# Two head groups of a gated delta rule: one joint triangular solve, two recurrences advanced in turn, and the output projection dealt between the backward steps

## The chip, the cores and the metric

The kernel runs on one core of a Trainium2 chip. The metric is the device time of one execution in microseconds (us). Three timed runs of the kernel before gave 1509.27, 1511.0 and 1515.41 us, so the median is 1511.0 us. The engines are TensorE (PE, with its weight loads shown apart as PEld), VectorE (DVE), ScalarE (ACT), GpSimd (POOL) and SyncE (SP), which issues nearly all DMA transfers.

## The reference, cut to what matters

Two layers, each for 128 context tokens and 1024 latent tokens of width 1024. One input projection feeds three branches: A, windowed attention with 8 query heads over 2 key heads; B, a gated MLP over 128-token chunks; C, a gated delta rule in both directions, with 4 heads of width 64. The three are concatenated, projected by `w_out`, normalised, gated and added to the residual. All tokens of layer 1 depend on layer 0. Branch C is what the change is about:

```python
a_mat = where(strict, einsum('bnihd,bnjhd->bnhij', kb, k) * decay, 0)   # one 64x64 block per chunk and head
t_mat = triangular_solve(a_mat + eye, eye, lower=True, unit_diagonal=True)
u, w  = t_mat @ (v * beta), t_mat @ (kb * exp(gc))
def step(state, xs):                       # one chunk of 64 tokens after the other
    v_new = uc - wc @ state
    o     = qd @ state + aqk @ v_new
    state = state * exp(gl) + kd.T @ v_new
    return state, o
# forward over chunks 0..15, backward over chunks 15..0; the context has 2 chunks and its own states
o = o_forward + flip(o_backward);  o = rmsnorm(o) * silu(gate)
mix = concat(o_a, o_b, o_c) @ w_out;  y = x + gate * rmsnorm(mix)
```

## The kernel before, in words

One large function, `hybrid_trunk`, writes all instructions out. Tile tracks the dependencies and orders each engine's instructions when it builds the program; priority follows the order in which the code emits them, so emission order is the kernel's main means of scheduling. On the chip each engine executes its list in order.

**Chain and fill.** For each layer, `merge` (L1107) interleaves two Python generators. `chain()` is branch C: features and gates (`c_features`, `c_gates`), then `scan`. `fill()` is everything else: `b_branch`, `c_gate` (the projection that gates branch C), and `attention`; `both()` adds `b_gate` for two column halves. Each `yield` carries a number, about the TensorE time in us of what was just emitted; a chain yield is scaled by a factor from `SHARE` and by `FILL` = 0.9, and that much fill is emitted after it. For instance a query tile of attention yields 5.2, one head's scores 0.95, a key/value tile 2.9, a `b_branch` tile 3.2, a `b_gate` tile 2.75, a block of `c_gate` 5.2. Layer 0's fill also holds the modulation of layer 1 (`mod`).

**`scan` (L419).** The four heads go in two head groups `hg` of two. A block position `p` is a pair of chunks, 8 latent positions and one context position (`CTX`); `r` is 0 for the first half of a recurrence and 1 for the second. `prep` (L429) makes the decay-weighted products of one position in both directions. `diagonals` (L469), `solve` (L493) and `inverses` (L506) invert the 64x64 blocks: VectorE solves 32x32 triangles by 31 rank-one steps of two instructions (L500 multiplies, L502 subtracts), TensorE joins them. Order in a layer: context preps of both groups; 8 preps of group 0, with the context solve between them; the solve of group 0; the 18 steps of group 0, with the 8 preps of group 1 between them; the solve of group 1; the 18 steps of group 1. `b_gate` 0 is released inside the first latent solve and `b_gate` 1 inside the second (the list `light`).

**A step** (`pre` L552, `post` L565). `pre` scales and transposes the queries and keys (PSUM bank `psw`, one buffer). `post` holds the one buffer of bank `psv` from its first matmul (L572) to the last read of it: matmuls L572 and L573, the copy `vn` by VectorE (L575), matmuls L577, L580 and L581, the state update L585 by VectorE, and the output to `oacc` (L588 by ScalarE or L590 by VectorE). `prep` uses both banks too. In the second half (r = 1), group 1's steps end with `c_final_norm` and, a step later, `c_final_out`, which write their rows of the concatenated branches to `mix_d` in HBM.

**`out_layer` (L1027)** comes after `merge`. It loads the last two of the four column blocks of `w_out` (the first two are loaded at steps 6 and 8 of group 1), then for each of nine token tiles reads `OTm` from `mix_d` and does 96 matmuls of 256 columns (L1055), the norm, the residual and, in layer 0, the normalised input of layer 1 (`make_h`). Its tiles are emitted in the order 3, 4, 2, 5, 1, 6, 0, 7, 8: the middle tiles' positions are the first that the second half of the recurrences finishes.

PSUM has 8 banks: three of `psp`, and one each of a, b, c (`psw`), v (`psv`) and o.

Of the kernel before, what the change touches and what calls it, by code (L numbers as in the profile page):

```python
# [26 lines left out]
CTX = 8  # L27
# [4 lines left out]
SHARE = ((1.08, 5.56, 1.88, 2.27, 5.93, 1.0, 2.13), (1.39, 4.8, 2.03, 2.16, 2.49, 1.87, 1.7))  # L32
BOOST = 0

WO_AT = 6
# [5 lines left out]
LT = 9  # L41
AHEAD = 4
FILL = 0.9
# [3 lines left out]
def hybrid_trunk(  # L47
# [227 lines left out]
    def make_h(hp, xn, t, AB, first=False):  # L275
        cond = 1 if t == CTX else 0
        hf = hp.tile([128, 8, 128], F32, tag="hf", name=nm("hf"))
        for hh in range(2):
            ps = psb() if hh else psa()
# [139 lines left out]
    def scan(l, cqk, cv_, gates, oacc, ng, NAc, keep, wo, light):  # L419
# [9 lines left out]
        def prep(ep, hg, NA, p):  # L429
# [12 lines left out]
            V.tensor_copy(hl[:, 0, :, 0], hl[:, 1, :, 0])  # L442
            V.tensor_copy(hl[:, 0, :, 1], hl[:, 2, :, 0])
# [25 lines left out]
        def diagonals(ep, W, L):  # L469
            D = ep[:, 0:64 * L].rearrange("p (n c) -> p n c", c=32)  # L470
# [10 lines left out]
            M = ep[:, 1024:2048]  # L481
            Dt = D.transpose([0, 2, 1])
            Mt = M.rearrange("p (r c) -> p c r", c=32)
            if L < 16:
                Dt = bc(Dt, 2, 16 // L)
                Mt = Mt.rearrange("p c (x y) -> p c x y", y=2 * L)
            V.transpose(Mt, Dt)
            Y = ep[:, 2048:3072]
            V.memset(Y, 0.0)
            V.memset(Y[:, 0:1024:33], 1.0)  # L490
            return M, Y

        def solve(ep, M, Y):  # L493
            m3 = M.rearrange("p (r c) -> p r c", c=32)
            y3 = Y.rearrange("p (r c) -> p r c", c=32)
            for m in range(31, 0, -1):
                tmp = ep[:, 3072:3328]
                w = 32 - m
                t3 = tmp[:, 0:m * w].rearrange("p (r c) -> p r c", c=w)
                V.tensor_tensor(t3, m3[:, 0:m, m:m + 1].to_broadcast([128, m, w]),  # L500
                                y3[:, m:m + 1, m:32].to_broadcast([128, m, w]), op=ALU.mult)
                V.tensor_tensor(y3[:, 0:m, m:32], y3[:, 0:m, m:32], t3, op=ALU.subtract)  # L502
                yield 1.0


        def inverses(ep, W, L, Y):  # L506
            PQ = []
            for f in range(2):
                P_ = ep[:, 1024 * f:1024 * f + 1024].rearrange("p (a b) -> p a b", b=32)
                V.transpose(P_.transpose([0, 2, 1]), Y.rearrange("p (r c) -> p c r" if f == 0 else "p (r c) -> p r c", c=32))  # L510
                PQ.append(P_)
# [7 lines left out]
            C_ = ep[:, 3328:3840]  # L519
            S_.activation(C_[:, 0:32 * L], ps[:, 0:32 * L], AF.Copy, scale=-1.0)  # L520
# [18 lines left out]
        def steps(hg, NA, sp, fp):  # L539
# [3 lines left out]
            def scaled(r, p):  # L543
                e2 = eg[:, 0, r, p, h0:h0 + 2]
                qk = sp.tile([128, 2, 2, 64], F32, tag="qk", name=nm("qk"), bufs=3)
                G.tensor_tensor(qk, Cqk[:, p].rearrange("p k (h d) -> p k h d", d=64), bc(bc(e2, 1, 2), 3, 64), op=ALU.mult)
                kd = sp.tile([128, 2, 64], F32, tag="kd", name=nm("kd"), bufs=4)
# [4 lines left out]
            def pre(r, p, qk, kd):  # L552
# [8 lines left out]
                qw = sp.tile([128, 2, 2, 64], F32, tag="qw", name=nm("qw"))  # L561
                S_.copy(qw.rearrange("p k h c -> p (k h c)"), ps[:, 0:256])
                return qw, kd

            def post(r, p, S, pr):  # L565
# [8 lines left out]
                vn = sp.tile([128, 2, 64], F32, tag="vn", name=nm("vn"))  # L574
# [7 lines left out]
                Sd = sp.tile([128, 2, 64], F32, tag="Sd", name=nm("Sd"))  # L582
                G.tensor_tensor(Sd, S, bc(eg[:, 2, r, p, h0:h0 + 2], 2, 64), op=ALU.mult)
                Sn = sp.tile([128, 2, 64], F32, tag="S", name=nm("S"), bufs=4)
# [8 lines left out]
            def swap(S):  # L593
                Sn = sp.tile([128, 2, 64], F32, tag="S", name=nm("Sx"), bufs=4)
                dma(Sn[0:64], S[64:128])
                dma(Sn[64:128], S[0:64])
                return Sn

            Sl = sp.tile([128, 2, 64], F32, tag="S", name=nm("S0"), bufs=4)
            for d in range(2):  # L600
                dma(Sl[64 * d:64 * d + 64], state_delta[0, l, d, h0:h0 + 2].rearrange("h d v -> d h v"))
            Sc = sp.tile([128, 2, 64], F32, tag="S", name=nm("Sc"), bufs=4)
# [655 lines left out]
```

## Time and profile before

| | before |
|---|---|
| median of three runs | 1511.0 us |
| the profiled execution, its own time | 1512.14 us |
| its span, first to last instruction | 1510.3 us |
| TensorE busy | 1324.8 us (88%) |
| VectorE busy | 971.8 us (64%) |
| ScalarE / GpSimd busy | 658.0 / 651.4 us |
| mean granted TensorE clock | 0.931 of full speed |

The profile is of one execution. Its page gives each engine's busy time, the wait before each group of instructions and what ended it, and the chain of work that ended last. A busy TensorE is not TensorE at its densest: the end of a matmul is modelled, and sparse small matmuls can count as busy. So the windows, which give the number of matmuls in a stretch beside the busy time, say more than the share on the page.

### The profile page before, as it was taken

The page shows a single profiled execution, that of the slowest core. Times are in us where ns is not written, and L with a number is a line of the kernel's source. Part 1 is how long each engine was busy: PE and PEld are TensorE (multiplying, and loading weights), DVE is VectorE, ACT ScalarE, POOL GpSimd, SP SyncE. Part 2 cuts the span into 40 slices and gives each one's busy share as a digit, 9 for nine tenths or more (in the row PEclk, how much of TensorE's full clock was granted, in tenths as well). Part 3 has the DMA queues.
Part 4 walks back from the last instruction along what each step waited for, and adds up shares of the span by engine and source line. Part 5 has one row for each costly group of instructions (what it writes and reads, how often), then busy time and mean ns, then how long its engine had stood idle before and what let it go on. Part 6 is the DMA issues. An engine that isn't in the chain of part 4 may idle for free.

```text
span 1510.3 us, 38004 instructions
## 1 busy us (share of the span) xinstructions
PE 1324.8 (88%) x15191; PEld 1014.2 (67%) x15191; DVE 971.8 (64%) x2446; ACT 658.0 (44%) x1483; POOL 651.4 (43%) x890
## 2 busy tenths in 40 slices
PE   6899978799988598888989998889987779977997
PEld 2764565566657487667877655778776668855887
DVE  2855789986556575764555766979765385756333
ACT  2733445624555315642443444443566314654211
POOL 0751156624565423662324335553566413656200
PEclk8999999999999889989998998999997789988999
DMA  9331044537864215666332112341556112756443
GB/s 357 104 93 37 23 105 121 125 116 189 170 163 88 42 50 122 114 174 171 128 114 60 58 36 83 83 102 40 96 113 95 34 52 64 143 94 164 128 156 110
DMA packets 301563, 162.91 MB, mean 108 GB/s; under 512 B 212622, under 2 KB 277938, under 8 KB 301386
## 3 DMA queue, kind: packets, MB, share of 16 engines
q1 hardware_dynamic: 301261, 160.45, 43.1%
q8 instruction: 119, 1.95, 0.5%
q14 instruction: 58, 0.48, 0.1%
q10 hardware_dynamic: 125, 0.04, 0.0%
HBM read 95.78 MB, written 24.28 MB: 79 GB/s over the span
## 4 chain that ended last, share of the span: by engine, by line
PE 48%; DVE 21%; DMA 12%; issue 7%; POOL 5%; ACT 5%; SPq 1%; DVEq 0%; POOLq 0%; ACTq 0%
PE ps L170 13%; PE ps L1055 11%; PE ps L312 7%; DMA PT<-P 4%; DMA st<-in_w_in_dram 3%; DVE sv L502 2%; DVE sv L500 2%; PE ps L249 2%; POOL P L934 2%; DVE sS L927 2%; PE ps L950 1%; DVE wg L161 1%; PE ps L533 1%; PE ps L517 1%; PE ps L698 1%
## 5 line engine op out<-in xcount | busy, mean ns | idle before, releaser
L170 PEld LDWEIGHTS <-X 128*128 128x128 f16 x3888 | 352.5, 101 | 108.4 <-issue 43.8
L170 PE MATMUL ps<-wg,X 128*128 128x256 f16 x2592 | 331.1, 281 | 14.8 <-DVE wg L161 4.4
L1055 PEld LDWEIGHTS <-OTm 128*128 128x128 f16 x1728 | 170.4, 100 | 38.1 <-DMA OTm<-mix_d 13.9
L934 POOL TENSOR_TENSOR P<-sS,P 128x512 f16<-128x512 f32 (+2 forms) x144 | 150.1, 1048 | 87.7 <-ACT sS L932 69.9
L1055 PE MATMUL ps<-wo,OTm 128*128 128x256 f16 x1296 | 155.1, 280 | 13.3 <-DMA OTm<-mix_d 12.7
L312 PE MATMUL ps<-X,wg 128*128 128x512 f16 (+1 forms) x864 | 145.7, 328 | 1.8 <-ACT wg L160 1.4
L931 ACT ACTIVATE P<-sS,nmx 128x512 f16<-128x512 f32 (+2 forms) x144 | 93.4, 659 | 89.6 <-DVE nmx L929 78.2
L312 PEld LDWEIGHTS <-wg 128*128 128x128 f16 x864 | 73.8, 99 | 68.5 <-ACT wg L160 1.8
L170 PE MATMUL ps<-wb,X 128*128 128x256 f16 x864 | 105.7, 284 | 12.2 <-DVE wb L161 6.2
L927 DVE CUSTOM_DVE_ANT_0 sS<-ps,am 128x512 f32<-128x512 f32 (+2 forms) x144 | 86.1, 609 | 35.2 <-PE ps L923 18.3
L950 PE MATMUL ps<-Vt,PT 128*128 128x128 f16 (+1 forms) x992 | 72.3, 215 | 34.5 <-DMA PT<-P 30.1
L932 ACT ACTIVATE sS<-sS,nmx 128x512 f32<-128x512 f32 (+2 forms) x144 | 94.7, 658 | 4.0
L145 POOL TENSOR_TENSOR rs<-ms,mhalf 128x1 f32<-128x1 f32 x36 | 19.8, 552 | 167.8 <-DVE ms L1064 89.7
L950 PEld LDWEIGHTS <-PT 128*128 128x128 f16 x992 | 51.9, 102 | 52.8 <-DMA PT<-P 43.7
L319 DVE SCALAR_TENSOR_TENSOR y<-zT,cw,y 128x1156 f32<-128x1156 f32 x48 | 68.9, 1438 | 28.3 <-ACT y L317 27.7
L502 DVE TENSOR_TENSOR sv<-sv 128x31 f32<-128x31 f32 (+15 forms) x186 | 77.3, 415 | 4.0
L500 DVE TENSOR_TENSOR sv<-sv 128x31 f32<-128x31 f32 (+15 forms) x186 | 74.0, 398 | 3.8
L923 PE MATMUL ps<-KT,qT 128*128 128x128 f16 (+2 forms) x272 | 71.2, 277 | 0.0
L922 PE MATMUL ps<-KT,qT 128*128 128x128 f16 (+2 forms) x272 | 62.3, 278 | 7.5 <-DMA qT<-ql 4.5
L161 DVE SCALAR_TENSOR_TENSOR wg<-st,wg 128x1024 f16<-128x1024 f32 x44 | 55.2, 1261 | 18.0 <-ACT wg L160 17.9
L160 ACT ACTIVATE wg<-st 128x1024 f16<-128x1024 f32 x44 | 45.2, 1054 | 46.3 <-DMA st<-in_w_in_dram 30.3
L1058 ACT ACTIVATE sq<-ps 128x512 f32<-128x512 f32 x36 | 21.3, 593 | 98.6 <-PE ps L1055 56.9
(272 smaller groups left out, 2861.9 us busy)
## 6 DMA issues: line engine op xcount, KB each, us to landing
st<-in_w_in_dram SPq DMA_DIRECT2D x40, 512.0 KB
st<-in_w_mod_dram SPq DMA_DIRECT2D x32, 512.0 KB
OTm<-mix_d SPq DMA_DIRECT2D x18, 512.0 KB
wm<-in_w_mod_dram SPq DMA_DIRECT2D x16, 512.0 KB
xt<-in_x_sample_dram SPq DMA_DIRECT2D x16, 512.0 KB
st<-in_w_out_dram SPq DMA_DIRECT2D x16, 512.0 KB
mix_d<-OTA SPq DMA_DIRECT2D x36, 128.0 KB
xs<-xt SPq DMA_DIRECT2D x9, 512.0 KB
```

What stands on the lines that cost most here:

```text
L161: V.scalar_tensor_tensor(dst[:, 4 * h:4 * h + 4, 1, :cols], s, WS, hi, op0=ALU.mult, op1=ALU.subtract)
L170: T.matmul(ps, X[:, t, k, a, :], wg[:, k, b, c0:c0 + n], start=(i == 0), stop=(i == 23))
L312: T.matmul(ps[:, 0:n], wg[:, k, b, 128 * hg:128 * hg + 128], X[:, t0:t1, k, a, :], start=(i == 0), stop=(i == 23))
L500: V.tensor_tensor(t3, m3[:, 0:m, m:m + 1].to_broadcast([128, m, w]), y3[:, m:m + 1, m:32].to_broadcast([128, m, w]), op=ALU.mult)
L502: V.tensor_tensor(y3[:, 0:m, m:32], y3[:, 0:m, m:32], t3, op=ALU.subtract)
L923: T.matmul(ps[:, cs], qT[:, h, :], Kl[:, kv, ks], start=False, stop=True)
L927: V.tensor_tensor_reduce(sS[:, 0:nk], ps[:, 0:nk], mk, 1.0, NEG, ALU.add, ALU.max, accum_out=mx[:, h:h + 1])
L931: S_.activation(P16[:, 0:nk], sS[:, 0:nk], AF.Exp, bias=nmx[:, h:h + 1], scale=0.125)
L932: S_.activation(sS[:, 0:nk], sS[:, 0:nk], AF.Exp, bias=nmx[:, h:h + 1], scale=0.125, accum_out=sm[:, h:h + 1])
L934: G.tensor_tensor(P16[:, nk:2 * nk], sS[:, 0:nk], P16[:, 0:nk], op=ALU.subtract)
L950: T.matmul(pops[:, 128 * h:128 * h + n], PT[:, a * nb + j, :], Vt[:, blist[j], kv].rearrange("p s d -> p (s d)")[:, 0:n], start=(i == 0), ...
L1055: T.matmul(ps[:, 256 * i:256 * i + 256], OTm[:, k, a, :], w[:, k, b, :], start=(n == 0), stop=(n == 23))
```

## The change

`scan` now does all 18 preps in a row (groups alternating), with the context solve between them. One `solve` runs both groups' latent blocks at once: its tiles have a further dimension of two, it has 30 rank-one steps instead of 31, and it works in place on the negated matrix (the sign moves into the copies at the head of `prep`), so that the separate result and its full memset are gone. `diagonals` and `inverses` still run once per group. Then the steps of both groups are emitted in turn, one of each per yield, 18 pairs. Each group has its own tags for its step tiles; banks c and v stay single. Context steps come first in each half.

`out_layer` becomes a generator at the end of the fill. A tile may be emitted once its positions are in the list `done`, which `c_final_out` fills; before that the generator yields `None`, and `merge` caps its credit at 6. The context tile goes first. All of `w_out` is loaded at its start. `c_gate` and both `b_gate` halves are the fill from the end of the preps on, and `merge` emits what is left of them before the steps begin. `SHARE` and `FILL` get new values, and the second buffer of `GG` goes.

```diff
-SHARE = ((1.08, 5.56, 1.88, 2.27, 5.93, 1.0, 2.13), (1.39, 4.8, 2.03, 2.16, 2.49, 1.87, 1.7))
+SHARE = ((1.08, 7.4, 2.1, 8.4), (1.39, 5.9, 2.1, 7.9))
-FILL = 0.9
+FILL = 1.0
...
-            V.tensor_copy(hl[:, 0, :, 0], hl[:, 1, :, 0])
+            V.tensor_scalar(hl[:, 0, :, 0], hl[:, 1, :, 0], -1.0, None, op0=ALU.mult)
...
+        def solve(Y, tmp, n):
+            y = Y.rearrange("p (s r c) -> p s r c", s=n, c=32)
+            for m in range(30, 0, -1):
+                w = 31 - m
+                t = tmp[:, 0:n * m * w].rearrange("p (s r c) -> p s r c", s=n, c=w)
+                V.tensor_tensor(t, y[:, :, 0:m, m:m + 1].to_broadcast([128, n, m, w]),
+                                y[:, :, m:m + 1, m + 1:32].to_broadcast([128, n, m, w]), op=ALU.mult)
+                V.tensor_tensor(y[:, :, 0:m, m + 1:32], y[:, :, 0:m, m + 1:32], t, op=ALU.add)
+                yield 1.0
...
+                    for i in range(16):
+                        prep(gp, i % 2, NAs[i % 2], i // 2)
+                        for _ in range(2):
+                            next(ctx_solve, None)
+                        yield share[1]
...
+                light.append(1)
+                for hg in range(2):
+                    diagonals(D[:, 1024 * hg:1024 * hg + 1024], Y[:, 1024 * hg:1024 * hg + 1024], Ws[hg], 16)
+                yield 4.0
+                for cost in solve(Y, D, 2):
+                    yield cost * share[2]
...
+                light.append(2)
+                yield 4.0
...
+                both = [steps(hg, NAs[hg], sp, fp, oacc) for hg in range(2)]
+                for _ in range(18):
+                    for s in both:
+                        next(s)
+                    yield share[3]
...
-            for ti, t in enumerate((3, 4, 2, 5, 1, 6, 0, 7, 8)):
+            for ti, t in enumerate((8, 3, 4, 2, 5, 1, 6, 0, 7)):
+                while not all(p in done for p in ((CTX,) if t == CTX else (min(2 * t, 15 - 2 * t), min(2 * t + 1, 14 - 2 * t)))):
+                    yield None
...
-                    g = p1.tile([128, DM], F32, tag="GG", name=nm("GG"), bufs=2)
+                    g = p1.tile([128, DM], F32, tag="GG", name=nm("GG"), bufs=1)
...
-                    ps = psp() if ti % 2 == 0 else (psw() if hh else psb())
+                    ps = psa() if ti % 2 and hh else psp()
...
-            while credit > 0:
-                c_ = next(fill, None)
+            while credit > 0 or len(light) == 2:
+                c_ = next(fill, -1)
                 if c_ is None:
-                    credit = -1e9
+                    credit = min(credit, 6.0)
+                    break
...
+            todo = [c_gate, lambda l, bp: b_gate(l, bp, 0), lambda l, bp: b_gate(l, bp, 1)]
```

## Rows read from the trace of the kernel before

**Rows 1.** The page's first part: busy us of each engine, share, instructions.

```profile
PE 1324.8 (88%) x15191; PEld 1014.2 (67%) x15191; DVE 971.8 (64%) x2446; ACT 658.0 (44%) x1483; POOL 651.4 (43%) x890
```

**Rows 2.** Windows of 20 us: busy (instructions) of five engines, clock, DMA.

```profile
1180.00:1200.00 20.00, 14.38 (x226) 12.56 (x224) 7.56 (x27) 4.91 (x13) 9.32 (x19) 0.57 0.18 34
1460.00:1480.00 20.00, 20.00 (x186) 17.93 (x184) 6.15 (x14) 2.75 (x8) 1.08 (x2) 1.00 0.54 172
...
400.00:420.00 20.00, 20.00 (x261) 13.78 (x259) 10.74 (x34) 10.07 (x28) 12.72 (x17) 1.00 0.76 165
```

**Rows 3.** Timeline of one step of layer 1: start us, us, engine, line.

```profile
1200.08 0.33 PE L580 MATMUL ps<-S,qw 64*64 64x64 f32 x4
...
1200.19 0.33 PE L581 MATMUL ps<-vn,NA 64*64 64x64 f32 x4
...
1206.09 0.34 PE L572 MATMUL ps<-cv,NA 64*64 64x64 f32 x4
...
1208.55 0.28 DVE L590 TENSOR_TENSOR oacc<-oacc,ps 128x128 f32<-128x128 f32 x1
```

**Rows 4.** The same windows, by stage of each layer.

```profile
75.00:205.00 130.00, 120.83 (x1048) 72.72 (x1046) 84.35 (x109) 53.13 (x90) 38.90 (x35) 0.99 0.21 57
205.00:306.00 101.00, 84.02 (x825) 61.54 (x824) 87.26 (x243) 53.52 (x142) 64.34 (x99) 0.92 0.52 123
306.00:377.00 71.00, 67.81 (x735) 47.53 (x737) 55.13 (x142) 27.02 (x60) 26.11 (x30) 0.95 0.58 149
377.00:521.00 144.00, 123.54 (x1830) 91.70 (x1822) 80.65 (x255) 75.12 (x186) 81.37 (x128) 0.97 0.55 119
521.00:577.00 56.00, 50.56 (x611) 43.66 (x612) 41.42 (x98) 12.24 (x23) 11.11 (x11) 0.86 0.19 54
577.00:663.00 86.00, 71.55 (x1188) 57.61 (x1187) 56.87 (x180) 52.73 (x132) 56.79 (x80) 0.94 0.65 122
663.00:795.00 132.00, 118.39 (x1195) 102.91 (x1193) 69.00 (x176) 49.20 (x93) 37.69 (x48) 0.95 0.50 152
795.00:926.00 131.00, 127.70 (x1107) 82.88 (x1105) 91.33 (x128) 54.97 (x88) 46.34 (x37) 0.95 0.21 59
926.00:1025.00 99.00, 87.92 (x868) 69.63 (x869) 77.34 (x199) 45.66 (x112) 54.45 (x89) 0.93 0.32 81
...
1092.00:1217.00 125.00, 98.23 (x1558) 79.37 (x1557) 65.73 (x206) 65.09 (x158) 73.44 (x119) 0.83 0.45 78
...
1281.00:1386.00 105.00, 88.99 (x1360) 71.56 (x1359) 69.94 (x221) 63.16 (x161) 68.59 (x93) 0.91 0.64 118
1386.00:1511.00 125.00, 109.25 (x1094) 94.45 (x1091) 44.48 (x104) 21.55 (x55) 15.55 (x24) 0.95 0.47 144
```

**Rows 5.** Groups of VectorE by line and shape: count, busy us, mean ns, idle before.

```profile
L465 DVE TENSOR_TENSOR NA<-ps,E 128x256 f32<-128x256 f32 x64 | 23.8, 412 | 13.4 <-POOL E L463 10.0 <-PE ps L454 3.3
L442 DVE COPY PK<-PK 128x128 f16<-128x128 f16 x36 | 10.2, 283 | 19.6 <-ACT PK L438 19.4
L500 DVE TENSOR_TENSOR sv<-sv 128x31 f32<-128x31 f32 x12 | 2.3, 194 | 0.2
L500 DVE TENSOR_TENSOR sv<-sv 128x256 f32<-128x256 f32 x6 | 3.2, 526 | 0.1
L510 DVE STREAM_TRANSPOSE sv<-sv 128x1024 f32<-128x1024 f32 x12 | 23.5, 2014 | 0.1
```

**Rows 6.** Windows of the state update L585 alone: one per step.

```profile
588.00:704.00 116.00, 5.08 (x18) 0.93 0.69 153
1296.00:1422.00 126.00, 5.05 (x18) 0.91 0.62 131
```

**Rows 7.** Timeline of the last step of layer 1 and the next output tile.

```profile
1421.06 0.28 DVE L590 TENSOR_TENSOR oacc<-oacc,ps 128x128 f32<-128x128 f32 x1
...
1437.68 1.15 PE L1055 MATMUL ps<-wo,OTm 128*128 128x256 f16 x7 [3.66 <-DMA OTm<-mix_d]
```

More of the change, by code (lines that the diff above doesn't have):

```diff
@@ L275, in make_h @@
     def make_h(hp, xn, t, AB, first=False):
+        hb = (lambda: psa()) if first else (lambda: bank("o", 1))
         cond = 1 if t == CTX else 0
@@ L416, in c_gates, with scan @@
         yield 6.0
-    def scan(l, cqk, cv_, gates, oacc, ng, NAc, keep, wo, light):
+    def scan(l, cqk, cv_, gates, ng, NAc, light, done):
         GB, eg, kdf, gh, gl = gates
@@ L617, in steps @@
                     if r == 0:
-                        Sc = swap(Sc)
+                        Sc = swap(Sc, p)
+                    else:
+                        for d in range(2):
+                            dma(new_s[0, l, 1 - d, h0:h0 + 2].rearrange("h d v -> d h v"), Sc[64 * d:64 * d + 64])
                 else:
@@ L640, in scratch @@
-        def scratch(p, tag=None):
-            return p.tile([128, 4096], F32, tag=tag, name=nm("sv")) if tag else p.tile([128, 3840], F32, name=nm("sv"))
-        def lat_solve(hg, sv):
-            M, Y = diagonals(sv, Ws[hg], 16)
-            yield 4.0
-            for i, cost in enumerate(solve(sv, M, Y)):
-                if i == (2 if hg else LT):
-                    light.append(hg)
-                yield cost * share[5 if hg else 2]
-            inverses(sv, Ws[hg], 16, Y)
-            yield 4.0
@@ L653, in scan @@
-        blocks(hp, "na")
-        with pool(f"gx{l}", 1) as cx, pool(f"gp{l}0", 2) as gp:
-            for i in range(2):
-                prep(gp, i, None, CTX)
-                yield share[1]
-            cx = scratch(cx)
-            M, Y = diagonals(cx, Wc, 4)
-            ctx_solve = solve(cx, M, Y)
-            for p in range(8):
-                prep(gp, 0, NAs[0], p)
-                for _ in range(4):
-                    next(ctx_solve, None)
-                yield share[1]
-            inverses(cx, Wc, 4, Y)
@@ L667, in scan @@
-        with pool(f"gv{l}", 1) as gv:
-            yield from lat_solve(0, scratch(gv))
-        hp1 = keep.enter_context(pool(f"ge{l}", 1))
-        blocks(hp1, "nb")
-        with pool(f"gp{l}1", 2) as gp, pool(f"gs{l}0", 2) as sp:
-            for i, cost in enumerate(steps(0, NAs[0], sp, None)):
-                cost *= share[3]
-                if i % 2 and i < 16:
-                    prep(gp, 1, NAs[1], i // 2)
-                    cost += share[4]
-                yield cost
-        yield from lat_solve(1, scratch(hp, "na"))
@@ L1105, in hybrid_trunk, with merge @@
             make_h(ph, xts[t], t, AB, True)
-    def merge(chain, fill):
+    def merge(chain, fill, light):
         credit = 0.0
@@ L1155, in chain @@
                     yield cost * SHARE[l][0]
-            yield from scan(l, cqk, cv_, gates, oacc, ng, NAc, keep, wo, light)
+            for cost in scan(l, cqk, cv_, gates, ng, NAc, light, done if OUTM else later):
+                yield cost
+            done.extend(later)
+        later = []
         def fill():
@@ L1160, in fill @@
                 yield from b_branch(l, vt, bp)
-            with pool(f"cg{l}", 1, "right") as cgp:
-                yield from c_gate(l, cgp)
             if l + 1 < NL:
@@ L1188, in hybrid_trunk @@
                 next(fl)
-        merge(chain(), fl)
+        merge(chain(), fl, light)
         rs.close()
-        out_layer(l, wo, nxt[1])
-        keep.close()
         ls.close()
```

168 lines of the change are left out of this document (82 added, 86 removed).

## The prediction, made before the changed kernel was run

> **What bounds the kernel now.** I read the page's first part, then windows cut at the stages of each layer, then the timeline of single steps. The page says TensorE is busy 88% of the span and VectorE 64% [rows 1], which looks like a kernel with 12% left to win. The windows say more. Where output tiles run alone, 186 matmuls of 256 columns fit in 20 us [rows 2]: 107.5 ns each, TensorE at its densest. The small fp32 matmuls of a step, issued closely, come four in 0.12 us, or 29 ns each [rows 3]. Giving every matmul of a stretch the dense time of its shape (107.5 ns per 256 columns and in proportion, 29 ns for the small ones) turns counts into "dense work": 1165 us for all 15,191, which is 77% of the span, against 88% busy. The rest, some 345 us, is room.
>
> By stage, dense work over length of the window [rows 4] is:
>
> - features: 119 of 130 us in layer 0, 123 of 131 in layer 1, so 0.92 and 0.94
> - first preps: 72 of 101 (0.71) and 79 of 99 (0.80). VectorE is busy 87 of the 101
> - latent solves, with `b_gate` beside them: 65 of 71 (0.91) and 45 of 56 in layer 0. Layer 1's stand between its rows' ends, 67 and 64 us long, at 0.84 and 0.81
> - steps of group 0 with the preps of group 1: 101 of 144 (0.70) and 66 of 125 (0.53)
> - steps of group 1: 56 of 86 and 67 of 105, both about 0.65
> - output, with the last steps still running: 110 of 132 (0.83) and 102 of 125 (0.82)
>
> The losses sit in the two stages of steps: 73 us in layer 0, 97 us in layer 1. Their worst form is a recurrence whose fill has run out. At 1180 to 1200 us TensorE is called busy for 14.4 us, holds 7 us of dense work, and has a granted clock of 0.57 of full speed, part of it at 1.2 GHz instead of 2.4 [rows 2]. The best form is attention rich in query tiles, 20 of 20 us busy at 400 to 420, 0.87 by dense work [rows 2]. No engine is full over the whole span; each stage loses to waits between small instructions, and what decides is whether the program has other matmuls to put there.
>
> On the 88%: the Trainium skill ("Perfetto Trace Analysis", Identifying the Most-Contended Engine) says that matmul busy is a poor measure of distance to the peak and that weight-load busy is a better one. Here weight loads are busy 67% [rows 1]. By the matmul share at most 185 us could be won, by the weight-load share 496; the 345 above lies between, and my sum goes by stages and needs neither.
>
> **The change part by part.** All matmuls stay, so I redistribute about 566 us of dense work per layer and give each new stage the density of the old stage most like it. Fill is counted in the yields' own us: 5.2 for a query tile is 48 matmuls x 107.5 ns.
>
> *Prologue*: unchanged, 75 us.
>
> *Features.* `c_gate` (23 us of dense work) leaves, key/value tiles and `b_branch` come in by credit: six features and 14 of gates at 1.08 give 22 of fill in layer 0, 28 at 1.39 in layer 1. The chain's own work is about 85. So 107 / 0.92 = 116 us and 113 / 0.93 = 121 us.
>
> *Preps.* 18 in a row, at 7.4 and 5.9: 133 and 106 of fill. A prep is about 1.0 us of TensorE (8 transposes and 14 products of 64 or 128 columns). Layer 0: 18 + 4 for the context inverses + 133 = 155 of dense work. VectorE: two copies of 0.3 and two L465 of 0.41 [rows 5] make 1.45 per prep, 26 us; the context solve 24 us (60 instructions of about 0.4, between the two rows of L500 [rows 5]); its transposes 8. The first preps before held ten preps, the context solve and 50 of fill in 87 us of VectorE [rows 4], which leaves 0.8 us per unit of fill, so 133 units need 106. Sum 164 us. VectorE is the tighter one here: at the 0.86 that it reached before, 190 us. Layer 1: 128 of dense work at 0.80 is 160 us, VectorE 134 / 0.86 = 156; I take 160. The negating copies replace plain copies of the same shape; a gain or loss of 0.1 us on 72 is 7 us either way and lies under the same 0.86.
>
> *Solve.* Instructions of 31 and 256 elements take 194 and 526 ns on average [rows 5]: 0.15 us and 1.48 ns per element. Two solves before: 124 instructions, 21,824 elements, 51 us. The joint one: 60 instructions, 19,840 elements, 38 us. With diagonals and inverses (three transposes of 2.0 us [rows 5] and some smaller copies per group) VectorE needs about 56 us. TensorE has 73 of fill (`c_gate` and both `b_gate` halves, all of which must be out before the steps) and 16 of joining matmuls: 89 / 0.90 = 99 us. So the solve, whatever it saves on VectorE, is hidden behind the gate projections; the two stages before took 127 and 131. Without that cover it would cost the 56.
>
> *Steps.* 36 turns per layer, 28 matmuls in two passes each: 56 x 29 ns = 1.6 us per turn. Bank v is still one buffer, so the groups take turns in it; a turn holds it from 1206.09 to 1208.83 [rows 3], about 3 us with little else on the engines. Under load, 18 steps took 116 and 126 us [rows 6], 6.4 and 7.0 us each. Side by side therefore buys no shorter chain by itself; what it buys is one place for all fill. Per pair 8.4 or 7.9 of fill go with 3.2 of steps, against 1.9 and 1.6 before in group 1's stage. First half: what is left of attention, 61 and 83, plus 28 of steps: 89 / 0.70 = 127 us and 111 / 0.70 = 159 us. That is 7.1 and 8.8 us per turn, at or above the rows.
>
> *Second half and output.* 94 of output tiles, 28 of steps, 4 of transposes: 126 / 0.83 = 152 us per layer, tail included. I keep the output stage's old density: tiles are dense and always ready, but after the last step norm, write and read of `mix_d` stay, 16.6 us from the last `oacc` to the next tile's first matmul [rows 7]. The loads of `w_out` are the same eight halves as before, now together after attention; the recurrences run beside them. Single-buffered `GG` delays one tile's epilogue, not its matmuls: nothing, as the next tile's 10 us cover it.
>
> *Sum.* Layer 0: 116 + 190 + 99 + 127 + 152 = 684 us (720 before, 75 to 795). Layer 1: 121 + 160 + 99 + 159 + 152 = 691 us (716 before). With 75 the span is 1450 us, 60 under 1510.3. The execution lay 1.8 us above its span and 1.1 us above the median, so against the median of 1511.0 I forecast **1450 us**, 4.0% less.
>
> **Bounds of the unknown.** No row shows attention beside two recurrences or output tiles beside backward turns from the start. First half: 0.53 to 0.87 gives 377 to 230 us for both layers against 286, so +91 to -56. Second half: 0.64 to 0.94 gives 394 to 268 against 304, so +90 to -36. Preps: 0.71 in both layers is +48; VectorE at 0.95 is -25. I take the middle densities because the fill per turn is four times that of the stages at 0.65, yet attention's own waits stay.
>
> **Rivals.**
>
> *Turns in one bank (slower).* If two recurrences and denser fill stretch a turn, the chain sets the steps' time. My sum allows 279 and 311 us for 36 turns, 7.8 and 8.6 us each. For it: 6.4 to 7.0 us per turn were reached with a quarter of the fill [rows 6]. Against it: a bare turn is 3 us. At 10 us per turn the steps take 720 us instead of 590, so 1580 us; slower than before from 9.1 us per turn on.
>
> *Tiles block the list (no gain).* A tile's matmuls stand in TensorE's list behind the step that frees them; if the read has not landed, both recurrences wait behind it. 16.6 us less a pair's 8.4 of fill is 8.2 us at four points in two layers: +66, 1516 us. For it: TensorE idled 3.66 us at such a point [rows 7]. Against it: the order is made from an estimate of readiness. The Trainium skill ("TensorE: Matmul & The Clock Gate", Step-by-step: what each phase is for) says that matmuls stay in program order while only weight loads are pulled ahead; by that rule nothing behind such a matmul could run. The row agrees as far as it goes: no other matmul ran in that gap.
>
> *Denser throughout (faster still).* First half 0.87, second 0.94: 1358 us. For it: the stretch at 400 [rows 2]. Against it: no long stretch with attention kept that.
>
> *It does not do what it says.* Tile may order the groups one after the other again, and the output last. Only the joint solve and the moved gates would stay, about 1505 us.
>
> **Chances.** Forecast, 1405 to 1495: 0.56. Denser, below 1405: 0.12. Blocked tiles, 1495 to 1519: 0.09, half of it under 1503. Not as said: 0.05. Turns, above 1519: 0.18. A difference under 0.5%, 7.5 us, can hardly be told from none. Faster 0.73, same 0.09, slower 0.18. The range is 1390 to 1525 us: it leaves about 0.05 below and 0.15 above.
>
> **What would show it.** Right: L585 in pairs, 13 to 17 us per pair; the joint L500 near 0.9 us at its widest; matmuls of the output tiles between L585 of the second half; TensorE at clock 1.0 through it; about 10 us of output matmuls alone per layer at the end. Wrong: gaps before L572 that bank v ends, or before L1055 that `OTm` ends, or VectorE full through the solve with TensorE waiting.

## The result and the profile after

The changed kernel takes 1581.98 us (median of four runs, 1579.81 to 1587.09) against 1510.43 us before on the same chip: a ratio of 1.0472, 95% interval 1.0437 to 1.0507. The forecast was 1450 us. The matmuls keep their form, but lines shift: the tile matmul L1055 is L1047 now, a step's L572, L577 and L585 are L569, L574 and L582, the solve's L500 is L495.

The page's first part answers [rows 1]: busy us of each engine, share of the span, instructions.

```profile
PE 1341.5 (85%) x15191; PEld 1026.5 (65%) x15191; DVE 955.8 (61%) x2308; ACT 657.2 (42%) x1483; POOL 663.8 (42%) x890
```

The same matmuls are called busy 17 us longer in a span 68 us longer. The windows of the changed kernel, one for each term of the sum (features, preps, solve, first half, second half with output, for layer 0 and then layer 1), answer [rows 4]; after the busy times of five engines stand clock, DMA share and GB/s.

```profile
75.00:232.00 157.00, 138.48 (x1217) 92.16 (x1216) 100.59 (x164) 63.64 (x129) 68.83 (x71) 0.92 0.26 67
232.00:385.00 153.00, 128.61 (x1264) 82.02 (x1262) 122.53 (x352) 96.86 (x230) 91.25 (x128) 0.94 0.73 167
385.00:525.00 140.00, 127.79 (x1381) 99.92 (x1381) 81.77 (x175) 40.65 (x91) 33.92 (x40) 0.90 0.32 84
525.00:649.00 124.00, 100.97 (x1692) 83.46 (x1690) 75.47 (x220) 69.96 (x174) 71.60 (x107) 0.93 0.65 128
649.00:855.00 206.00, 164.16 (x1918) 139.82 (x1919) 82.26 (x228) 54.31 (x109) 56.57 (x86) 0.86 0.29 87
855.00:1003.00 148.00, 133.35 (x1194) 91.97 (x1193) 102.89 (x151) 61.06 (x109) 68.32 (x65) 0.96 0.22 58
1003.00:1140.00 137.00, 111.47 (x1209) 87.95 (x1208) 118.19 (x340) 88.92 (x218) 88.43 (x130) 0.93 0.40 78
1140.00:1265.00 125.00, 111.23 (x1237) 87.26 (x1235) 84.13 (x163) 41.04 (x85) 33.09 (x30) 0.83 0.35 91
1265.00:1397.00 132.00, 118.49 (x1849) 100.08 (x1846) 71.16 (x227) 64.90 (x174) 74.92 (x118) 0.96 0.48 89
1397.00:1578.00 181.00, 152.46 (x1892) 127.71 (x1892) 72.10 (x193) 39.33 (x101) 47.24 (x74) 0.92 0.41 119
```

Set against the sum, both layers together: features and preps 595 us, forecast 587 (+8); solve 265, forecast 198 (+67); first half 256, forecast 286 (-30); second half and output 387, forecast 304 (+83). These make the 128 us between 1450 and 1578, the span. Dense work, counted as in the prediction, is 132 of 206 us (0.64) and 128 of 181 us (0.70) in the last stage, where 0.83 was assumed.

What such a stage looks like is in the timeline of TensorE in layer 0: start, duration, line; in brackets the idle time before and what ended it.

```profile
698.23 0.33 PE L578 MATMUL ps<-vn,NA 64*64 64x64 f32 x4
704.57 4.24 PE L1047 MATMUL ps<-wg,OTm 128*128 128x256 f16 x24 [6.01 <-DMA OTm<-mix_d]
708.65 2.78 PE L1047 MATMUL ps<-wo,OTm 128*128 128x256 f16 x24
...
719.13 2.78 PE L1047 MATMUL ps<-wo,OTm 128*128 128x256 f16 x24
721.84 0.34 PE L569 MATMUL ps<-cv,NA 64*64 64x64 f32 x4
```

A step ends at 698.6. Next in TensorE's order stand six blocks of 24 tile matmuls, and the first waits 6 us for its read of `mix_d`, whose rows of branch C an earlier step had to finish. The next step starts at 721.84. In between, neither recurrence moves, and so no new position is finished: tile and step take turns instead of overlapping. The first block after the gap takes 4.24 us, the others 2.78. At the end the last tile waits for the last step. The tail of layer 0 answers [rows 7]. TensorE idles 8.4 us before L281, the transposes with which `make_h` turns a finished tile into layer 1's input: with no other tile free they stand next in its order, and wait for that tile's norm.

```profile
814.95 0.44 PE L716 MATMUL ps<-ident,on 128*128 128x128 f32 x2 [0.23 <-DVE hf L288]
823.79 1.97 PE L281 MATMUL ps<-ident,xn 128*128 128x128 f32 x8 [8.41 <-ACT xn L272]
826.17 4.87 PE L1047 MATMUL ps<-wg,OTm 128*128 128x256 f16 x24 [0.41 <-DMA OTm<-mix_d]
```

The chain that ended last shows that this idle time lies inside a longer wait: the read of the last tile, issued behind the write of its rows, lands just before that tile's first matmul (start, length, step of the chain).

```profile
820.00 1.82 DMA mix_d<-oc
821.84 4.28 DMA OTm<-mix_d
```

Before that, once attention had run out (its last matmul ran at 624) and until the first tile was free (670), both recurrences ran bare; this window, with the first tile in it, answers the first of [rows 2]:

```profile
613.00:700.00 87.00, 57.58 (x970) 48.73 (x969) 33.76 (x90) 25.21 (x57) 31.31 (x59) 0.80 0.41 109
```

It holds 37 us of dense work in 87, 10 of them the first tile, at a granted clock of 0.80: part of it at 1.2 GHz.

### The profile page after: what moved, and what is told of

It reads as the page before. It is cut to its first block, busy times and chain, and to the rows that moved or that the text cites. A ratio compares the mean times of both kernels' runs of the same rounds, so it can differ in the third digit from the quotient of the medians.

```text
span 1578.0 us, 37851 instructions
## 1 busy us (share of the span) xinstructions
PE 1341.5 (85%) x15191; PEld 1026.5 (65%) x15191; DVE 955.8 (61%) x2308; ACT 657.2 (42%) x1483; POOL 663.8 (42%) x890
## 5 line engine op out<-in xcount | busy, mean ns | idle before, releaser
L169 PE MATMUL ps<-wg,X 128*128 128x256 f16 x2592 | 324.8, 278 | 12.6 <-DVE wg L160 5.8
L921 POOL TENSOR_TENSOR P<-sS,P 128x512 f16<-128x512 f32 (+2 forms) x144 | 154.3, 1078 | 133.1 <-ACT sS L919 89.8
L1047 PEld LDWEIGHTS <-OTm 128*128 128x128 f16 x1728 | 172.3, 101 | 51.4 <-DMA OTm<-mix_d 24.6
L312 PE MATMUL ps<-X,wg 128*128 128x512 f16 (+1 forms) x864 | 151.6, 335 | 17.4 <-ACT vf L991 9.5
L1047 PE MATMUL ps<-wg,OTm 128*128 128x256 f16 x864 | 114.8, 292 | 22.6 <-DMA OTm<-mix_d 22.6
L1047 PE MATMUL ps<-wo,OTm 128*128 128x256 f16 x864 | 103.1, 274 | 0.0
L160 DVE SCALAR_TENSOR_TENSOR wg<-st,wg 128x1024 f16<-128x1024 f32 x44 | 58.5, 1343 | 35.5 <-ACT wg L159 35.4
L540 POOL TENSOR_TENSOR qk<-cqk,eg 128x256 f32<-128x256 f32 x72 | 46.0, 639 | 48.4 <-PE ps L553 48.3
L495 DVE TENSOR_TENSOR sv<-sv 128x168 f32<-128x168 f32 (+28 forms) x120 | 64.8, 540 | 1.6
```

Of the source, the lines that this page charges most:

```text
L169: T.matmul(ps, X[:, t, k, a, :], wg[:, k, b, c0:c0 + n], start=(i == 0), stop=(i == 23))
L312: T.matmul(ps[:, 0:n], wg[:, k, b, 128 * hg:128 * hg + 128], X[:, t0:t1, k, a, :], start=(i == 0), stop=(i == 23))
L495: V.tensor_tensor(t, y[:, :, 0:m, m:m + 1].to_broadcast([128, n, m, w]), y[:, :, m:m + 1, m + 1:32].to_broadcast([128, n, m, w]), op=ALU.mult)
L921: G.tensor_tensor(P16[:, nk:2 * nk], sS[:, 0:nk], P16[:, 0:nk], op=ALU.subtract)
L1047: T.matmul(ps[:, 256 * i:256 * i + 256], OTm[:, k, a, :], w[:, k, b, :], start=(n == 0), stop=(n == 23))
```

## Experiments

Each kernel was timed beside the kernel before on the same chip; the number in parentheses is its ratio to before with the 95% interval. Unless said otherwise the edit is made on the changed kernel (1582 us).

**Is it the dealing?** Three edits: tiles after all steps, steps ahead of the tiles in the list, and tiles that wait for nothing.

```diff
-OUTM = 1
+OUTM = 0        # `done` is filled only after all 36 steps are emitted
```

> Changed: the dealing alone is undone. An output tile is released only when all 36 steps have been emitted, so in the lists every step comes before every tile unless the scheduler finds a gap for the tile. Theory A (list order): dealt tiles stand in TensorE's list as whole blocks of 96 matmuls ahead of the next steps, so tiles and steps take turns instead of overlapping; the second half with the output took 215 and 190 us after against 154 and 153 before, and this should win back 60 to 100 us of these 98: 1480 to 1520 us. Theory B (late tiles): the tiles come late because a tile now needs the second half of both groups, and the recurrences run bare before that; no order of the list helps: 1570 to 1600 us.

Measured: 1539.72 us (1.0191, 1.0159 to 1.0222). 42 us come back, less than expected of theory A and more than of B. Dealing is one loss among others.

```diff
-BOOST = 0
+BOOST = 400
...
-            tc.cur_priority = at - BOOST
+            ahead = BOOST if len(light) == 3 else 0
+            tc.cur_priority = at - ahead
...
-            tc.cur_priority += BOOST
+            tc.cur_priority += ahead
```

> Changed: the instructions of the steps get a priority 400 places ahead of the fill that was emitted before them; the dealing stays. In TensorE's list steps then stand inside the blocks of tile matmuls, mostly one step to 40 or 50 matmuls. Theory A (list order): 60 to 100 us less, 1480 to 1520 us, like the kernel without dealing. Theory B (late tiles): 1570 to 1600 us.

Measured: 1567.5 us (1.0379, 1.034 to 1.0418), 15 us less. Steps now stand inside the blocks, and the idle time before tiles is still 14.9 us (22.6 in the changed kernel, 12.7 before). Order of the list alone is not enough.

```diff
-            dma(mix_d[ch // 2, :, 6:8, :, 64 * (ch % 2):64 * (ch % 2) + 64], oc[:, i])
+            dma(oc_d[ch // 2, :, :, :, 64 * (ch % 2):64 * (ch % 2) + 64], oc[:, i])
...
-                dma(OTm, mix_d[t])
+                dma(OTm[:, 0:6], mix_d[t, :, 0:6]); dma(OTm[:, 6:8], mix_d[t, :, 4:6])
```

> Changed: the output tiles no longer depend on branch C. Its rows go to a memory of their own and the tiles read other rows in their place, so the output leaves branch C out. The tiles are still dealt between the steps, and each is emitted where it was. The sum of the prediction took second half and output at 152 us per layer because tiles are always ready. If readiness is what failed: 152 to 165 us per layer and 1480 to 1520 us in all. If the turns in one bank and steps behind tiles cost as much with ready tiles: 1545 to 1580 us.

Measured: 1507.59 us (0.9954, 0.9916 to 0.9992), 74 us less. Its second halves with the output, from the 18th state update of each layer:

```profile
651.00:787.00 136.00, 132.27 (x1799) 113.74 (x1795) 74.64 (x215) 50.79 (x103) 55.32 (x86) 1.00 0.44 128
1338.00:1508.00 170.00, 148.62 (x1892) 126.09 (x1892) 72.39 (x193) 39.51 (x101) 48.02 (x74) 0.94 0.44 127
```

136 + 170 = 306 us, where the prediction had 304 and the changed kernel 387. With tiles that wait for nothing the step of the prediction holds for the two layers together, one bank v and all; what failed in it is that tiles are ready. Singly the layers lie 16 us under and 18 over their 152; in layer 1 attention ran on to 1372, into this stage. And readiness changes the list too: in layer 0 no more than 39 tile matmuls stand here between two matmuls of steps, where the changed kernel has four blocks of 96 to 144. This run does not separate the wait from that order.

**Is it that a tile needs both groups?**

```diff
-                for _ in range(18):
-                    for s in both:
+                for j, s in enumerate(both):
+                    for i in range(18):
                         next(s)
-                    yield share[3]
+                        yield share[3] * ((0.27, 0.39)[l] if 18 * j + i < 27 else 1.2)
```

> Changed: the recurrences alone. Group 0 does its 18 steps, then group 1, as before the change; the joint solve, all preps in a row and the dealt tiles stay, and the rest of attention is spread over the first 27 steps. Theory B (late tiles): nine steps instead of eighteen stand between the first free tile and the last, and each two tiles come free after two steps instead of four: 60 to 100 us less than the changed kernel, 1480 to 1520 us. Theory A (list order): the tiles are dealt ahead of the next steps here too, in blocks that a step cannot enter; group 1's nine steps wait behind them, but there are half as many: 1535 to 1565 us.

Measured: 1637.92 us (1.0835, 1.0795 to 1.0875), 56 us more. Theory B falls: with half as many steps left when tiles come free, the kernel is slower still, and up to 192 tile matmuls now run between two steps of the only recurrence (TensorE's timeline from 737 to 761 and 779 to 804 us in layer 0, 1512 to 1535 and 1545 to 1569 in layer 1). Without dealing:

> Changed: groups one after the other (as in the run of 1638 us) and no dealing. What stays of the change is the joint solve, all preps in a row and the moved gate projections. If the blocks of dealt tiles in front of steps made that run slow (theory A), this is 70 to 130 us under it: 1505 to 1565 us. If a single recurrence without preps beside it is the loss, it stays over 1590 us. Against the undealt kernel with the groups in turn (1540 us) the difference is the worth of side by side in one bank: I expect 0 to 30 us more here.

Measured: 1553.7 us (1.027, 1.023 to 1.031), 84 us less than dealt, and 14 more than with the groups in turn. So side by side is worth 14 us in one bank, and the blocks of tiles are what made the run before slow. And this kernel, which keeps of the change the joint solve, the preps in a row and the moved gates, is 45 us slower than before, where the prediction gave it 1505 us.

**Is it the one bank v?**

```diff
-        return bank("p", 3)
+        return bank("p", 2)
...
-    def psv():
-        return bank("v", 1)
+    def psv(hg=0):
+        return bank(f"v{hg}", 1)
...
-                vso = psv()
+                vso = psv(hg)
```

> Changed: each group has its own bank v (taken from the three shared banks of the fill, which become two). Theory C (turns in one bank): the two recurrences wait for each other in bank v; with two banks a pair's turns overlap, and the bare stretches of 3.5 us per turn shrink by a third to a half: 30 to 60 us less, 1520 to 1550 us. Theories A and B: the chain is not what the loss is, within 15 us of the changed kernel (1567 to 1597 us), the missing third bank costing up to 15 more.

Measured: 1531.43 us (1.0133, 1.0101 to 1.0165), 50 us less, as theory C has it; but the place is another. Beside attention the first 18 state updates of layer 0 take 86 us in place of 113 (changed kernel first, then two banks):

```profile
536.00:649.00 113.00, 89.97 (x1541) 74.13 (x1535) 69.24 (x198) 63.38 (x159) 63.71 (x94) 0.93 0.66 132
```

```profile
548.00:634.00 86.00, 80.39 (x1470) 66.59 (x1466) 55.28 (x178) 52.61 (x141) 58.71 (x89) 0.98 0.60 112
```

In layer 1 they take 92 us in place of 114. Of these 49 us some 14 are dense work that now stands elsewhere. The bare turns are little shorter: layer 1's updates at 1393.8, 1396.8, 1399.9 and 1403.0 with one bank, at 1384.0, 1386.6, 1390.8 and 1392.4 with two, 3.1 and 2.8 us apart on average. What changes is the order, as the matmul L574 of two neighbouring steps shows, first with one bank, then with two:

```profile
566.38 0.45 PE L574 MATMUL ps<-vn,kd 64*64 64x64 f32 x8
...
573.60 0.45 PE L574 MATMUL ps<-vn,kd 64*64 64x64 f32 x8
```

```profile
588.05 0.45 PE L574 MATMUL ps<-vn,kd 64*64 64x64 f32 x8
...
589.27 0.45 PE L574 MATMUL ps<-vn,kd 64*64 64x64 f32 x8
```

With one bank a piece of attention stands between the two steps, which come 7.2 us apart; with two, both groups' steps pass together, 1.2 us apart, and the wait for `vn` is covered once per pair: TensorE's idle time before L574 goes from 18.5 to 6.9 us over the whole span.

The same edit on the kernel before, in its preps as well:

> Changed, on the kernel before: two banks v by group, in steps and preps, and two shared banks instead of three. There group 1's preps run beside group 0's steps in the one bank, and never two recurrences. If the second bank pays because two recurrences stand side by side: within 10 us of before, 1500 to 1520 us. If it pays in any stage of steps: 1470 to 1495 us.

Measured: 1516.3 us (1.0043, 1.0014 to 1.0071): a little slower. Where only one recurrence runs at a time, the second bank pays nothing.

**Two banks and no dealing together.**

> Changed: two banks v and no dealing, both at once. Two banks alone gave 1531 us and undealing alone 1540 us, 50 and 42 less than the changed kernel. If these are two losses (turns that wait for the bank; tiles that block the list) they add: 1480 to 1500 us, faster than before. If both are the same loss, the alternation of steps and tiles, taken away in two ways: 1520 to 1540 us.

Measured: 1500.43 us (0.9935, 0.9905 to 0.9966). Of 92 us, 82 come: nearly two separate losses. The end of layer 0 there, first the 18 updates of the second half, then the output behind them:

```profile
634.00:709.00 75.00, 59.88 (x1136) 51.22 (x1132) 36.23 (x108) 22.51 (x54) 37.19 (x63) 0.86 0.51 121
709.00:804.00 95.00, 91.61 (x841) 82.09 (x838) 54.02 (x135) 40.79 (x71) 27.44 (x30) 1.00 0.43 144
```

The recurrences finish 100 us earlier than in the changed kernel (709 against 809) and the tiles follow at clock 1.00, 91 us of dense work in 95. TensorE waits 0.0 us for `OTm`. Nothing but the next layer waits for tiles; kept for the end they are dense, dealt early they hold up the chain that frees them.

**Is the bare stretch a loss of its own?**

```diff
-                for _ in range(18):
+                for i in range(18):
...
-                    yield share[3]
+                    yield share[3] if i > 9 else (6.1, 8.3)[l]
```

> Changed: the shares of the pairs alone. What is left of attention (61 and 83 us) is spread over ten pairs, to the first free tile, in place of 8.4 and 7.9 us per pair until it is gone. Theory B' (bare stretch: pairs 7 to 11 find neither attention nor tiles): the bare 87 us of layer 0 and 70 us of layer 1 shrink and 15 to 35 us are won: 1545 to 1567 us. If the stretch is set by how the steps and tiles alternate later: within 10 us of 1582.

Measured: 1577.49 us (1.0417, 1.0366 to 1.0469). Hardly: 4 us, within the spread of either kernel's runs.

> Changed: two banks v, no dealing, and attention spread over ten pairs. By the theory of the bare stretch it is 10 to 25 us under the kernel with the first two edits; if with those two no step is bare any more, the same within 8 us.

Measured: 1507.94 us (0.9999, 0.9974 to 1.0025), rather 7 us more than without the spread.

**The joint solve and the moved gates.** Two solves in place of the joint one:

```diff
-                for cost in solve(Y, D, 2):
-                    yield cost * share[2]
+                for hg in range(2):
+                    for cost in solve(Y[:, 1024 * hg:1024 * hg + 1024], D, 1):
+                        yield cost * share[2] / 2
```

> Changed: the joint solve alone is undone, two solves of one group each, one behind the other in the same place, 120 instructions instead of 60 for the latent blocks; by the instructions' lengths that is 13 us more of VectorE per layer. The prediction held the solve hidden behind the gate projections: within 10 us of the changed kernel, 1575 to 1592 us. If VectorE sets the end of that stage: 1600 to 1612 us.

Measured: 1582.32 us (1.0442, 1.0389 to 1.0495): no difference. The solve is hidden, as forecast. But the cover need not stand there; in this edit `c_gate` goes back and the solve's share of fill falls, both at once:

```diff
-SHARE = ((1.08, 7.4, 2.1, 8.4), (1.39, 5.9, 2.1, 7.9))
+SHARE = ((1.08, 7.4, 1.4, 8.4), (1.39, 5.9, 1.4, 7.9))
...
             with pool(f"bp{l}", 2, "right") as bp:
                 yield from b_branch(l, vt, bp)
+            with pool(f"cg{l}", 1, "right") as cgp:
+                yield from c_gate(l, cgp)
...
-            todo = [c_gate, lambda l, bp: b_gate(l, bp, 0), lambda l, bp: b_gate(l, bp, 1)]
+            todo = [lambda l, bp: b_gate(l, bp, 0), lambda l, bp: b_gate(l, bp, 1)]
```

> Changed, on the changed kernel itself: c_gate back in the features' fill, solve's share 1.4. If the moved gate projection cost layer 0's features 15 to 20 us, 1560 to 1572 us; if the solve now lacks the cover of c_gate and loses as much, 1575 to 1590 us.

Measured: 1538.7 us (1.0163, 1.01 to 1.0226), 43 us less, twice what I expected, and not where I expected it. The features keep their length. The stretch from the first latent solve instruction (L495) to the first step shrinks, from 146 and 135 us in the changed kernel to 120 and 101:

```profile
390.00:536.00 146.00, 134.42 (x1518) 106.12 (x1517) 82.99 (x192) 43.86 (x101) 40.89 (x52) 0.92 0.33 82
1148.00:1283.00 135.00, 121.56 (x1390) 99.22 (x1389) 80.63 (x164) 41.59 (x89) 39.24 (x49) 0.85 0.31 84
```

```profile
399.00:519.00 120.00, 105.64 (x1256) 87.05 (x1255) 71.81 (x140) 34.30 (x70) 35.52 (x43) 0.82 0.31 82
1127.00:1229.00 102.00, 93.26 (x1256) 80.31 (x1254) 73.94 (x152) 33.49 (x71) 36.41 (x44) 0.95 0.29 75
```

It holds some 32 and 17 us less dense work: `c_gate`'s 23, and what the share moves. With `c_gate` in the features, other fill goes into the preps, some 17 us in layer 0 and 4 in layer 1, and into the steps. From the features' last matmul to that instruction the preps take 195 and 173 us, against 185 and 177: VectorE was busy for 122.5 of 153 us there in layer 0, and TensorE had room. In the changed kernel that work stood between the preps and the first step, where everything waits for it. How much of the 43 us is `c_gate` and how much the share was not separated.

> Changed, on the kernel with two banks v and no dealing (1500 us): c_gate goes back into the fill of the features, as before the change, and the solve's share goes from 2.1 to 1.4 so that attention is not pulled forward. Layer 0's features took 138 us there for 114 of dense work, against 112 for 109 before. If c_gate's dense projections were what filled them: 10 to 25 us less, 1475 to 1490 us. If not: 1495 to 1510 us.

Measured: 1495.13 us (0.9861, 0.9804 to 0.9917): only 5 us less here.

> Changed: groups one after the other, no dealing, c_gate back in the features' fill with the solve's share at 1.4. Of the change there remain the joint solve, which is worth nothing by the run with two solves, and all preps in a row. If the moved c_gate is what made the same kernel without this edit 44 us slower than before (1554 us): 1505 to 1520 us. If preps in a row cost it: 1535 to 1555 us.

Measured: 1552.78 us (1.0287, 1.0227 to 1.0347), as without this edit. So it is not the moved `c_gate` that makes that arrangement slower than before. What is left of it are the preps in a row, and behind them one recurrence without preps beside it; which of the two it is was not separated.

**How the three edits add up.** Two more kernels complete the table ("`c_gate` back" is with the lower share):

> Changed: one bank v as in the change, no dealing, c_gate back. Undealing alone gave 42 us, c_gate back alone 43. If they are two losses: 1490 to 1505 us. If c_gate back helped because attention then lasts longer beside the steps, so that fewer steps stand bare or behind tiles, the two gains overlap: 1515 to 1540 us.

Measured: 1519.6 us (1.0054, 1.003 to 1.0078).

> Changed: two banks v, c_gate back, tiles dealt. Two banks alone gave 50 us, c_gate back 43. If they are two losses: 1480 to 1500 us. If they overlap as they did without dealing (1500 to 1495 us): 1515 to 1535 us.

Measured: 1532.55 us (1.0155, 1.0128 to 1.0182).

| us | `c_gate` moved | `c_gate` back |
|---|---|---|
| one bank, dealt | 1582 (the change) | 1539 |
| one bank, not dealt | 1540 | 1520 |
| two banks, dealt | 1531 | 1533 |
| two banks, not dealt | 1500 | 1495 |

Dealing costs 19 to 42 us in every pair. Bank and gates overlap: with two banks and dealt tiles, `c_gate` back brings layer 0's last state update from 765 to 720 us, and the last tile matmul still ends the layer at 829. What is won ahead is lost again behind.

**A version that beats both.** In the kernel of 1495 us attention lasted to the last step of layer 1, the loads of `w_out` came only then, and the 35 us from 1360 on hold 16 of dense work. New shares for layer 1 end it earlier:

```diff
-SHARE = ((1.08, 7.4, 1.4, 8.4), (1.39, 5.9, 1.4, 7.9))
+SHARE = ((1.08, 7.4, 1.4, 8.4), (1.39, 6.4, 1.5, 9.5))
```

> Changed, on the kernel with two banks, no dealing and c_gate back (1495 us): layer 1's shares for preps, solve and pairs from 5.9, 1.4, 7.9 to 6.4, 1.5, 9.5. In layer 1 attention lasted to the last step there, the loads of w_out came after it, and TensorE held 13 us of dense work in the 35 us behind it. Ended earlier, attention leaves the last steps to the tiles: 10 to 20 us less, 1475 to 1487 us. If that gap moves elsewhere: 1490 to 1500 us.

Measured: 1471.57 us (0.9759, 0.9732 to 0.9785), 2.4% faster than before. Its second half and output of layer 0 take 176 us and of layer 1 172 us:

```profile
615.00:694.00 79.00, 72.03 (x1333) 60.98 (x1331) 54.29 (x161) 39.74 (x94) 47.30 (x73) 1.00 0.71 162
694.00:791.00 97.00, 91.08 (x812) 80.88 (x809) 54.52 (x133) 41.41 (x73) 28.59 (x32) 0.97 0.44 145
...
1298.00:1364.00 66.00, 57.38 (x1208) 48.07 (x1205) 51.27 (x157) 35.77 (x86) 47.06 (x72) 0.96 0.66 148
1364.00:1470.00 106.00, 96.59 (x870) 85.35 (x868) 34.39 (x75) 16.80 (x46) 11.32 (x17) 0.97 0.48 147
```

> Changed, on the tuned kernel (1472 us): the tiles are dealt again. With two banks dealing cost 31 and 38 us before the tuning. If steps held behind tiles are the loss whatever the shares: 1495 to 1515 us. If it came from the late attention of layer 1: within 10 us of 1472 us.

Measured: 1532.24 us (1.0146, 1.0109 to 1.0183). Dealing costs 61 us here, and its timeline shows it most plainly:

```profile
1398.68 0.33 PE L570 MATMUL ps<-S,qw 64*64 64x64 f32 x4
...
1400.92 3.67 PE L1047 MATMUL ps<-wg,OTm 128*128 128x256 f16 x24
...
1452.00 2.78 PE L1047 MATMUL ps<-wo,OTm 128*128 128x256 f16 x24
1454.71 0.45 PE L574 MATMUL ps<-vn,kd 64*64 64x64 f32 x8
```

Between the steps' first matmuls and the next L574 stand twenty blocks of tiles, 54 us, all dense. What L574 needs was there: GpSimd's last `kd` by 1387.2, and VectorE's copies `vn` before the second of these blocks:

```profile
1400.54 0.28 DVE L572 COPY vn<-ps 128x128 f32<-128x128 f32 x1
1401.06 0.28 DVE L572 COPY vn<-ps 128x128 f32<-128x128 f32 x1
```

Then the recurrences go on, and in the 73 us to the end TensorE is busy for 51. In the tuned kernel those blocks come last instead. The groups of TensorE that begin a tile's matmuls, and those of `make_h`, show the waits that dealing brings (idle time before the group and what ended it stand last): in the changed kernel, then tuned and dealt, then tuned.

```profile
L1047 PE MATMUL ps<-wg,OTm 128*128 128x256 f16 x864 | 114.8, 292 | 22.6 <-DMA OTm<-mix_d 22.6
L281 PE MATMUL ps<-ident,xn 128*128 128x128 f32 x72 | 13.0, 336 | 8.6 <-ACT xn L272 8.6
```

```profile
L1047 PE MATMUL ps<-wg,OTm 128*128 128x256 f16 x864 | 112.7, 291 | 20.0 <-DMA OTm<-mix_d 18.6 <-ACT wg L159 0.9 <-DVE wg L160 0.4
L281 PE MATMUL ps<-ident,xn 128*128 128x128 f32 x72 | 13.1, 342 | 21.3 <-ACT xn L272 21.3
```

```profile
L1047 PE MATMUL ps<-wg,OTm 128*128 128x256 f16 x864 | 104.3, 276 | 1.8 <-DMA OTm<-mix_d 1.8
L281 PE MATMUL ps<-ident,xn 128*128 128x128 f32 x72 | 11.1, 301 | 1.5 <-ACT xn L272 1.5
```

Of the 61 us, the growth of these two waits makes 38, if none of it lies beside another loss, which was not tested. As I read it: with two tiles free at a time there is no third to stand between a tile and its own `make_h`, or between a step and the read of its tile; with all nine left there is.

(The Trainium skill, "TensorE: Matmul & The Clock Gate", Step-by-step: what each phase is for, says that matmuls keep program order; the timeline agrees: both `vn` were there at 1401.3, and L574 ran at 1454.71, behind the tile matmuls.)

## Why the prediction was wrong

- **Second half and output, 152 us per layer: this is the step that failed.** It rests on "tiles are dense and always ready". They are dense once they run; they are not ready, and dealing made them less so, since a tile ahead of a step delays the next tile. Measured 206 and 181 us, +83 together. With tiles that wait for nothing, 306 against my 304, though by layer 136 and 170. In layer 1 a second thing is in it: I had attention over by then, and it ran on to 1430, 33 us into the stage, with the first tile at 1439.
- **Solve, 99 us per layer: second failure, +67.** VectorE was hidden, as said (two solves cost nothing). But I costed `c_gate`'s move at nothing beyond its dense time, and credited 0.90. The stage held 113 and 95 us of dense work in place of 89, at 0.81 and 0.76: other fill stood there too, and all of it lay ahead of the first step. Some 30 us of that work I had counted in other stages, 18 of them in the first half.
- **First half, 127 and 159 us:** measured 124 and 132, 6.9 and 7.3 us per turn. Right in kind; layer 1 had less to do.
- **Features and preps, 306 and 281 us:** measured 310 and 285, but that is luck in part. The windows give features 157 and 148 against 116 and 121, preps 153 and 137 against 190 and 160: +68 and -60, which cancel. The preps begin, at 194 in layer 0, before the features' last convolution, at 223; cut at the features' last matmul (206 and 971) the four are 131, 116, 179 and 169. VectorE was busy for 0.80 and 0.86 of the preps' windows, where I put 0.86. The two negating copies take 335 and 322 ns where the plain ones took 283 [rows 5] and 344, 1 us over all 72, inside the 7 that I allowed.
- **"Tiles block the list", 0.09, +66 us:** the right mechanism with too small a chance, and priced by the wrong part. Waiting for `OTm` grew by only 10 us (12.7 to 22.6), and I had not thought of `make_h` (0.8 before, 8.6 after, in layer 0's tail beside the read of the last tile). The rest fits steps held behind tiles that run perfectly well, which the timelines show; its price was not measured by itself. Together 42 us, 61 in the tuned kernel.
- **"Turns in one bank", 0.18, 1580 us:** the time agrees by chance. Turns did not come to 10 us; 36 took 273 and 248 us, 7.6 and 6.9 each (single gaps in the second half reach 30, where tiles stand between), and the waits that bank v ends sum to 3.7 us. The bank costs 50 us all the same, by keeping the two groups' steps apart in TensorE's order. I looked for it as a wait; it was an order.
- **"It does not do what it says", 1505 us:** the change did what it says. Its price was wrong too: that arrangement takes 1554 us.
- **What was to show it:** two state updates take 13 to 18 us beside attention, but not in pairs, as the single ones come 4 to 11 us apart; the solve's widest row takes 0.65 us, not 0.9; tiles do stand between second-half updates. Clock 1.0 in the second half was 0.86 and 0.92; ten us of tiles alone at the end were 40 in layer 0 and 39 in layer 1.
- **The working:** three figures do not come out of their rows, and none of them made the miss. The two dense times as stated give about 1110 us for all matmuls, not 1165 (features of layer 0 before 109 to 114, not 119); before and after are counted alike. "Fill per turn four times" sets a pair against a single step; per turn it is 4.2 and 4.0 against 1.9 and 1.6. VectorE at 0.95 shortens the preps by 17 us in layer 0, or 36 with layer 1, not 25.

## What to carry to other kernels

Before dealing ready-made fill between the steps of a chain, ask what the fill waits for: if the same chain frees it, whatever is put ahead of a step also delays the fill behind it, and such fill cost less after the chain's end (1540 against 1582 us). Fill that is ready does well between the steps (1508 us, branch C left out of it). A single buffer shared by two chains may show no wait at all and still cost, by forcing the two to alternate in an in-order engine; compare the distance between their instructions, not only the waits. Cover for a stage is not free because it is hidden there: price what must finish before the next stage begins, and try the movable part where another engine is the fuller one.

## What was not expected of the hardware

The first block of 24 tile matmuls after a gap took 4.24 us and 4.87 us where the next took 2.78. TensorE had been idle for 6.0 and 8.4 us, with one group of transposes before the second. The granted clock in the first of these blocks and in those behind it:

```profile
704.00:709.00 5.00, 4.43 (x28) 3.36 (x29) 0.00 (x0) 0.00 (x0) 0.00 (x0) 0.64 0.22 92
709.00:722.00 13.00, 13.00 (x123) 11.49 (x122) 3.07 (x7) 2.05 (x5) 0.55 (x1) 1.00 0.00 1
```

Part of the first block ran at 1.2 GHz, so a round of waiting is paid again in the block behind it, here with 1.5 and 2.1 us.

The joint solve's widest instruction, 480 elements, took 648 ns, while one of 240 in the context solve, beside the preps, took 861 ns; why was not tried.
